# Mixture-of-experts stage: the token scatter, the token gather and the sigmoid issued in other places between the weight steps

## The chip, the cores and the metric

The kernel runs on one core of one Trainium2 chip. Its engines work side by side, each through its own queue in order: TensorE (PE; its weight loads are shown as PEld), VectorE (DVE), ScalarE (ACT), GpSimd (POOL) and SyncE (SP), which here only issues DMAs. The metric is the time of one execution in microseconds, lower is better. All numbers are float32.

## The reference, cut to what matters

One transformer block on 256 tokens of width 2048: a modulated norm, one input projection, two kinds of chunked attention, an output projection, then a two-level mixture of experts and a final modulated norm. The part that the change touches is the mixture:

```python
for e in range(N_EXPERTS):                      # 32 experts, width 512 each
    a = jax.nn.silu(t @ w_gate[e]) * (t @ w_up[e])
    y = y + combine[:, e:e + 1] * (a @ w_down[e])
x = x + gt2 * y
```

Each token has two experts, so `combine` is zero nearly everywhere. The weights of the experts, three matrices of 4 MB for each, are most of what the kernel reads.

## The kernel before

**Weights.** Every large weight goes through one ring of six SBUF buffers of 2 MB (class `Ring`). A list fixes the order of all transfers ahead of time. `release` (called when the last matmul that reads a buffer has been issued in the program) lets SP issue the transfer that takes this buffer next (line 72); on the chip that issue waits until the matmuls have really been done.

**Experts.** They are taken in eight groups of four (line 894). A group has twelve steps of two ring buffers: for J = 0 to 3 a gate step and an up step (`gate_up`, line 773, four experts side by side in four column strips of TensorE), then four down steps fc = 0 to 3 (`down`, line 795). So a group is 24 transfers. Group 7 has eight down steps of one buffer each.

**Around the steps.** Each expert takes 32 slots. `place` (lines 724 and 729, DVE) makes a 0/1 matrix token to slot; `gather` (four `gather_part`s, lines 737 to 748) multiplies the tokens with it on TensorE, and DVE and ACT scale the result into `xg`, the left side of the gate and up matmuls. `activate` (lines 780 to 789) is the gate's silu: exponential on ACT, three operations on DVE, the product with the up result, four transposes on TensorE and a copy by ACT. `gated` (line 804) scales the down result on DVE, `scatter_matrix` (lines 758 to 766) makes the weighted matrix slot to token, and `scatter` (lines 811 and 813) multiplies with it on TensorE and adds into `x1` on DVE.

**Order.** It is written out by hand; every engine follows the order of the program. In each group: the eight gate and up steps, with the whole scatter of the group before behind the two steps of J = 0; then the place and the whole gather of the next group; then `activate`; then the four down steps, `gated` and the `scatter_matrix` of the next group. Group 0 also has `spread` of the gate vector (line 717) and its own `scatter_matrix` ahead of the gather, its scatter at its end, and behind that `further_rounds`, a branch (line 845) that is not taken with these inputs. Its own gather stands in four parts ahead of its first steps. Group 7 has no next group; behind its J = 1 and J = 2 it makes `gscf`, a scale for the final norm (lines 915 to 920). Small results go through a PSUM tag `m` of two banks.

Of the kernel before, what the change touches and what calls it, by code (L numbers as in the profile page):

```python
# [16 lines left out]
F32 = mybir.dt.float32  # L17
I32 = mybir.dt.int32
AF = mybir.ActivationFunctionType
ALU = mybir.AluOpType  # L20
# [21 lines left out]
ROW_ADA, ROW_FIN, ROW_MIX, ROW_FFN, ROW_GFIN, ROW_OA, ROW_OB = 0, 24, 32, 36, 40, 44, 46  # L42
# [42 lines left out]
def block_kernel(ctx: ExitStack, tc: tile.TileContext, a: dict):  # L85
# [72 lines left out]
    pr = const.tile([128, 512], F32, name="pr")  # L158
# [31 lines left out]
    def pick(r, m):  # L190

        return ident[:, r : r + 1].to_broadcast([128, m])
# [25 lines left out]
    with ExitStack() as sa:  # L218
# [181 lines left out]
        def spread(r, dst):  # L400
            for J in range(4):
                pm = bank("m", "pm_bc", 1)
                PE.matmul(pm, lhsT=pick(32 * J, 128), rhs=r, start=True, stop=True)
                S.copy(dst[:, J * 512 : (J + 1) * 512], pm)
# [305 lines left out]
    def mbank(tag, name, bufs):  # L710
        return psb.tile([128, 512], F32, tag=tag, name=name, bufs=bufs)

    def spread(r, row, dst, n=4):

        for J in range(n):
            pm = mbank("m", "bc", 2)
            PE.matmul(pm, lhsT=pick(32 * J, 128), rhs=r, start=True, stop=False)
            PE.matmul(pm, lhsT=pick(row + J, 128), rhs=pr, start=False, stop=True)
            S.copy(dst[:, J * 512 : (J + 1) * 512], pm)
# [12 lines left out]
    def gather_part(xg, pn, q, name):  # L732
        pm = mbank("m", f"g{q}_{name}", 2)
        for i in range(4):
            kk = 4 * q + i
            for t in range(2):
                PE.matmul(  # L737
                    pm[:, i * 128 : (i + 1) * 128], lhsT=big[:, t, kk * 128 : (kk + 1) * 128], rhs=pn[:, t, :],
                    start=t == 0 and i == 0, stop=t == 1, skip_group_check=True,
                )  # L740
        for i in range(4):
            kk = 4 * q + i
            if i % 2:
                S.activation(xg[:, kk, :], pm[:, i * 128 : (i + 1) * 128], AF.Identity, bias=sh2c[:, kk : kk + 1], scale=gsc2[:, kk : kk + 1])  # L744
            else:
                V.tensor_scalar(  # L746
                    xg[:, kk, :], pm[:, i * 128 : (i + 1) * 128], gsc2[:, kk : kk + 1], sh2c[:, kk : kk + 1], op0=ALU.mult, op1=ALU.add
                )

    def gather(pn, name):  # L750
        xg = pb.tile([128, 16, 128], F32, tag="xg", name=f"xg_{name}")
        for q in range(4):
            gather_part(xg, pn, q, name)
        return xg

    def scatter_matrix(pt, cb, name):
        pw = pb1.tile([128, 2, 4, SLOTS], F32, tag="placew", name=f"pw_{name}")
        V.tensor_tensor(pw, pt, cb.unsqueeze(3).to_broadcast([128, 2, 4, SLOTS]), op=ALU.mult)
        return turned(pw.rearrange("p t e c -> p t (e c)"), name)
# [16 lines left out]
                )  # L776

    def activate(gp, up, name):
        act = pb1.tile([128, 512], F32, tag="act", name=f"act_{name}")
        S.activation(act, gp, AF.Exp, scale=-1.0)  # L780
        V.tensor_scalar(act, act, 1.0, None, op0=ALU.add)
        V.reciprocal(act, act)  # L782
        V.tensor_tensor(act, act, gp, op=ALU.mult)  # L783
        V.tensor_tensor(act, act, up, op=ALU.mult)  # L784
        pm = mbank("m", f"at_{name}", 2)
        aT = pb1.tile([128, 4, 128], F32, tag="actT", name=f"actT_{name}")
        for c in range(4):
            PE.transpose(pm[:, c * 128 : (c + 1) * 128], act[:, c * 128 : (c + 1) * 128], ident)  # L788
        S.copy(aT.rearrange("p c n -> p (c n)"), pm)
        return aT  # L790
# [13 lines left out]
            V.tensor_tensor(ys[:, n, :], yp[n], gt2bc[:, c : c + 512], op=ALU.mult)  # L804
        return ys

    def scatter(sm, ys, ch, name, last=False):
        for n in range(2):
            for t in range(2):
                pm = mbank("m", f"sc_{name}{ch}{n}{t}", 2)  # L810
                PE.matmul(pm, lhsT=sm[:, t * 128 : (t + 1) * 128], rhs=ys[:, n, :], start=True, stop=True)  # L811
                c = slice(ch * 1024 + n * 512, ch * 1024 + (n + 1) * 512)
                V.tensor_tensor(x1[:, t, c], x1[:, t, c], pm, op=ALU.add)  # L813
                if last:
                    S.activation(rl, x1[:, t, c], AF.Square, accum_out=ss3[:, t, 2 * ch + n : 2 * ch + n + 1])
                    G.tensor_tensor(big[:, t, c], x1[:, t, c], gscf[:, c], op=ALU.mult)  # L816
# [72 lines left out]

    four = pb1.tile([128, 2], F32, name="four")  # L890
    V.tensor_reduce(four[:, 0:1], ident[:, 0:128:32], axis=AX.X, op=ALU.add)
    xg = pb.tile([128, 16, 128], F32, tag="xg", name="xg_g0")
    gather_part(xg, pn, 0, "g0")
    for g in range(8):
        gu, dn = moe_tiles[g]
        gp, up = mbank("g", f"gp{g}", 1), mbank("u", f"up{g}", 1)
        for J in range(4):
            if g == 0 and J < 3:
                gather_part(xg, pn, J + 1, "g0")
            for i, pbk in ((0, gp), (1, up)):  # L900
                pair = gu[2 * J + i]
                gate_up(pbk, xg, [ring.get(idx) for idx in pair], J)
                for idx in pair:
                    ring.release(idx)
            if J == 0:
                for job in pending:
                    scatter(*job)
                pending = []
            if g == 7 and J >= 1 and J < 3:
                if J == 1:  # L910
                    gscf = pb.tile([128, 16, 128], F32, tag="xg", name="gscf").rearrange("p k n -> p (k n)")
                for b in (2 * J - 2, 2 * J - 1):
                    c = slice(b * 512, (b + 1) * 512)
                    pm = mbank("m", f"gf{b}", 2)
                    PE.matmul(pm, lhsT=pick(ROW_GFIN + b, 128), rhs=pr, start=True, stop=True)
                    S.copy(gscf[:, c], pm)
                    pm = mbank("m", f"sf{b}", 2)
                    PE.matmul(pm, lhsT=pick(32 * b, 128), rhs=R["scf"], start=True, stop=False)
                    PE.matmul(pm, lhsT=pick(ROW_FIN + 4 + b, 128), rhs=pr, start=False, stop=True)
                    V.scalar_tensor_tensor(gscf[:, c], pm, 1.0, gscf[:, c], op0=ALU.add, op1=ALU.mult)  # L920
        if g == 0:
            spread(R["gt2"], ROW_ADA + 20, gt2bc)
            sm = scatter_matrix(pt, comb[:, :, 0:4], "g0")
        if g < 7:
            pt, pn = place(posk[:, :, 4 * g + 4 : 4 * g + 8], f"g{g + 1}")
            xg = gather(pn, f"g{g + 1}")
        aT = activate(gp, up, f"g{g}")
        if g == 7:
            S.activation(four[:, 1:2], four[:, 0:1], AF.Sqrt)
            rl = pb1.tile([128, 512], F32, tag="act", name="rl")  # L930
        if g < 7:
            yp = [mbank("y", f"yp{g}{n}", 4) for n in range(4)]
            for fc in range(4):
                pair = [ring.get(idx) for idx in dn[fc]]
                down(yp, aT, lambda e: pair[e // 2][:, e % 2, :], fc)
                for idx in dn[fc]:
                    ring.release(idx)
            pending = [(sm, gated(yp[2 * ch : 2 * ch + 2], ch, f"g{g}"), ch, f"g{g}") for ch in range(2)]
        else:
            for ch in range(2):  # L940
                yp = [mbank("y", f"yp{g}{ch}{n}", 4) for n in range(2)]
                for fc in range(4):
                    w = ring.get(dn[ch * 4 + fc])
                    down(yp, aT, lambda e: w[:, e, :], fc)
                    ring.release(dn[ch * 4 + fc])
                    if fc == 1 and ch == 1:
                        for job in pending:
                            scatter(*job)
                        pending = []
                    if fc == 1 and ch == 0:  # L950
                        shbc = pb.tile([128, 16, 128], F32, tag="xg", name="shbc").rearrange("p k n -> p (k n)")
                        spread(R["shf"], ROW_FIN, shbc, 2)
                pending.append((sm, gated(yp, ch, f"g{g}"), ch, f"g{g}", True))
        if g < 7:
            sm = scatter_matrix(pt, comb[:, :, 4 * g + 4 : 4 * g + 8], f"g{g + 1}")
        if g == 0:
            for job in pending:
                scatter(*job)
            pending = []
            further_rounds()  # L960
# [67 lines left out]
```

## Time and profile before

| | |
|---|---|
| time, median of 3 runs | 1560.95 us (1560.94 to 1568.42) |
| profiled execution, its time | 1562.42 us |
| its span, first to last instruction | 1560.7 us |
| TensorE matmul busy | 1181.1 us (76%) |
| VectorE busy | 462.6 us (30%) |
| ScalarE busy | 163.8 us (10%) |
| DMA | 599.40 MB, mean 384 GB/s |
| mean granted TensorE clock | 0.891 |

The profile is one execution on the chip. All times inside it count from its first instruction. The granted clock is that of TensorE as a share of 2.4 GHz: 1.00 is that level, 0.50 is 1.2 GHz, and a number between the two means that a stretch held both. A DMA share of 1.00 means that all 16 DMA engines were busy all the time; GB/s says what they moved. Line numbers are those of the kernel before.

### The profile page before, as it was taken

How to read it: one execution, taken by the hardware profiler on the slowest of the kernel's cores; microseconds unless marked ns; L12 is line 12 of the kernel's file. 1: busy time of each engine (PE TensorE's matmuls, PEld its weight loads, DVE VectorE, ACT ScalarE, POOL GpSimd, SP SyncE). 2: the span in 40 equal slices, each digit the busy share in tenths (PEclk: the TensorE clock that was granted, in tenths of full speed). 3: DMA queues.
4: the chain of work that ended last, by engine and by line, in shares of the span. 5: the costliest groups of instructions: out<-in, count | busy, mean ns of one | idle time of the engine just before them, and what ended most of it. 6: DMA issues, size and time to landing. Idle time of an engine off the chain costs nothing.

```text
span 1560.7 us, 14477 instructions
## 1 busy us (share of the span) xinstructions
PE 1181.1 (76%) x6073; PEld 533.7 (34%) x6074; DVE 462.6 (30%) x773; ACT 163.8 (10%) x420; POOL 142.7 (9%) x144
## 2 busy tenths in 40 slices
PE   4999999998989975765567577667657667567866
PEld 1657874873334541311211211211211121131211
DVE  1002667667697730220201201021021022022013
ACT  2101222131310110100100100100000010010001
POOL 0000433332332100000000000000000000000002
PEclk9999999998999988887788888878879888888889
DMA  9999999979799859799999999999999999999998
GB/s 353 390 392 389 352 335 363 373 292 382 300 379 399 332 224 422 313 385 411 422 402 422 421 392 422 421 389 421 421 412 421 421 394 421 422 390 421 421 388 333
DMA packets 128494, 599.40 MB, mean 384 GB/s; under 512 B 5832, under 2 KB 8440, under 8 KB 81064
## 3 DMA queue, kind: packets, MB, share of 16 engines
q1 hardware_dynamic: 124432, 593.51, 95.0%
q10 hardware_dynamic: 3960, 4.88, 0.9%
q8 instruction: 49, 0.80, 0.2%
q14 instruction: 21, 0.17, 0.0%
q0 software_dynamic: 32, 0.02, 0.0%
HBM read 596.02 MB, written 2.12 MB: 383 GB/s over the span
## 4 chain that ended last, share of the span: by engine, by line
DMA 34%; PE 16%; DVE 3%; ACT 1%; issue 0%; SPq 0%; DVEq 0%; ACTq 0%
DMA ring<-w_up 21%; DMA ring<-w_gate 9%; PE yp L795 5%; PE up L773 4%; DMA ring<-w_down 3%; PE gp L773 2%; PE g_g L737 2%; DMA ring<-w_ada_final 1%; DVE act_g L782 1%; ACT xg_g L744 1%; DVE xg_g L746 1%; PE sc_g L811 0%; PE at_g L788 0%; DVE act_g L783 0%; DVE act_g L784 0%
## 5 line engine op out<-in xcount | busy, mean ns | idle before, releaser
L773 PE MATMUL up<-ring,xg_g 128*32 128x512 f32 x1024 | 198.1, 808 | 120.3 <-DMA ring<-w_up 120.3
L773 PE MATMUL gp<-ring,xg_g 128*32 128x512 f32 x1024 | 169.5, 731 | 72.5 <-DMA ring<-w_gate 66.3
L795 PE MATMUL yp<-ring,actT_g 128*32 128x512 f32 x1024 | 156.3, 742 | 53.2 <-DMA ring<-w_down 47.4
L746 DVE TENSOR_SCALAR xg_g<-g_g,gsc,sh2c 128x128 f32<-128x128 f32 x64 | 26.3, 410 | 428.5 <-PE g_g L737 411.5
L773 PEld LDWEIGHTS up<-ring,xg_g 128*32 128x32 f32 x1024 | 43.4, 139 | 266.1 <-DMA ring<-w_up 155.0
L582 PE MATMUL po<-ring,oT 128*128 128x512 f32 x256 | 115.6, 607 | 0.0
L773 PEld LDWEIGHTS gp<-ring,xg_g 128*32 128x32 f32 x1024 | 39.6, 128 | 189.6 <-DMA ring<-w_gate 92.3
L816 POOL TENSOR_TENSOR big<-x,gscf 128x512 f32<-128x512 f32 x8 | 10.0, 1278 | 983.9 <-DVE x L813 983.9
L795 PEld LDWEIGHTS yp<-ring,actT_g 128*32 128x32 f32 x1024 | 36.3, 130 | 167.5 <-issue 91.5
L813 DVE TENSOR_TENSOR x<-x,sc_g 128x512 f32<-128x512 f32 x64 | 44.0, 687 | 152.2 <-PE sc_g L811 152.2
L744 ACT ACTIVATE xg_g<-g_g,sh2c,gsc 128x128 f32<-128x128 f32 x64 | 29.3, 458 | 538.6 <-DVE xg_g L746 538.6
L804 DVE TENSOR_TENSOR ys_g<-yp,gt2bc 128x512 f32<-128x512 f32 x32 | 22.1, 692 | 195.0 <-PE yp L795 195.0
L365 DVE SCALAR_TENSOR_TENSOR acc_gt<-ring,cact,acc_gt 128x1024 f32<-128x1024 f32 x60 | 78.7, 1312 | 1.9
L582 PEld LDWEIGHTS po<-ring,oT 128*128 128x128 f32 x256 | 48.9, 195 | 61.1 <-issue 61.1
L737 PE MATMUL g_g<-pn_g,big 128*128 128x128 f32 x512 | 64.3, 286 | 2.9 <-DVE pn_g L729 1.3
L737 PEld LDWEIGHTS g_g<-pn_g,big 128*128 128x128 f32 x512 | 61.1, 199 | 11.9 <-issue 8.8
L811 PE MATMUL sc_g<-ys_g,smat_g 128*128 128x512 f32 x128 | 61.7, 617 | 0.0
L549 PE MATMUL pw_vB<-ring,hT 128*128 128x512 f32 x128 | 58.4, 614 | 1.5 <-DMA ring<-w_in 1.5
L553 PE MATMUL pw_kB<-hT,ring 128*128 128x256 f32 x256 | 56.6, 381 | 0.0
L553 PE MATMUL pw_qB<-hT,ring 128*128 128x256 f32 x256 | 56.5, 381 | 0.0
L553 PEld LDWEIGHTS pw_qB<-hT,ring 128*128 128x128 f32 x256 | 48.2, 190 | 7.7 <-issue 1.0
L553 PEld LDWEIGHTS pw_kB<-hT,ring 128*128 128x128 f32 x256 | 48.2, 190 | 7.7 <-issue 0.7
(331 smaller groups left out, 1122.6 us busy)
## 6 DMA issues: line engine op xcount, KB each, us to landing
ring<-w_gate SPq DMA_DIRECT2D x64, 2048.0 KB
ring<-w_up SPq DMA_DIRECT2D x64, 2048.0 KB, 20.1
ring<-w_down SPq DMA_DIRECT2D x64, 2048.0 KB, 20.3
ring<-w_ada SPq DMA_DIRECT2D x32, 2048.0 KB, 10.3
ring<-w_in SPq DMA_DIRECT2D x18, 2048.0 KB, 13.0
ring<-w_ada SPq DMA_DIRECT2D x32, 1024.0 KB, 13.8
ring<-w_ada_final SPq DMA_DIRECT2D x15, 2048.0 KB, 8.9
ring<-w_out SPq DMA_DIRECT2D x8, 2048.0 KB, 14.4
```

The costliest lines, as they stand in the source:

```text
L365: V.scalar_tensor_tensor(acc, w[:, kk, :], cact[:, c : c + 1], acc, op0=ALU.mult, op1=ALU.add)
L549: PE.matmul(b[s], lhsT=hT[:, kk, s * 128 : (s + 1) * 128], rhs=w[:, k, :], start=kk == 0, stop=kk == 15)
L553: PE.matmul(b[s][:, n * 256 : (n + 1) * 256], lhsT=w[:, k, c * 128 : (c + 1) * 128], rhs=hT[:, kk, :], start=kk == 0 and n == 0, stop=kk = ...
L582: PE.matmul(b, lhsT=oT[:, (i // 4) * 8 + k, t * 128 : (t + 1) * 128], rhs=w[:, k, :], start=k == 0, stop=k == 7)
L737: PE.matmul(pm[:, i * 128 : (i + 1) * 128], lhsT=big[:, t, kk * 128 : (kk + 1) * 128], rhs=pn[:, t, :], start=t == 0 and i == 0, stop=t == ...
L744: S.activation(xg[:, kk, :], pm[:, i * 128 : (i + 1) * 128], AF.Identity, bias=sh2c[:, kk : kk + 1], scale=gsc2[:, kk : kk + 1])
L746: V.tensor_scalar(xg[:, kk, :], pm[:, i * 128 : (i + 1) * 128], gsc2[:, kk : kk + 1], sh2c[:, kk : kk + 1], op0=ALU.mult, op1=ALU.add)
L773: PE.matmul(bankt[32 * e : 32 * e + 32, :], lhsT=xg[:, kk, 32 * e : 32 * e + 32], rhs=w[e // 2][:, e % 2, j, :], start=kk == 0, stop=kk == ...
L795: PE.matmul(y[32 * e : 32 * e + 32, :], lhsT=aT[:, fc, 32 * e : 32 * e + 32], rhs=w(e)[:, n * 512 : (n + 1) * 512], start=fc == 0, stop=fc ...
L804: V.tensor_tensor(ys[:, n, :], yp[n], gt2bc[:, c : c + 512], op=ALU.mult)
L811: PE.matmul(pm, lhsT=sm[:, t * 128 : (t + 1) * 128], rhs=ys[:, n, :], start=True, stop=True)
L813: V.tensor_tensor(x1[:, t, c], x1[:, t, c], pm, op=ALU.add)
```

## The change

The gather of the next group and the scatter of the last one are issued in pieces, one behind each step, through a list `steps` of twelve entries. For groups 1 to 6 the four quarters of the scatter stand behind steps 0 to 3, `place` behind step 3, the four parts of the gather behind steps 4, 5, 6 and behind the first down step (entry 7). In group 0 the four parts of `spread` stand behind steps 3 to 6, `place` behind step 6, and the gather parts one behind each down step; there is no scatter from a group before. In group 7 the four parts of the final scale stand behind steps 3 to 6. `activate` is cut in two: `silu` stands behind the last gate step, ahead of the last up step; `combined` (product, transposes, copy) stands where `activate` stood. `scatter_matrix` of each group stands at the head of its loop turn; for groups 2 to 7 that is the same place on every engine as before (the end of the turn before), for group 1 it is now behind group 0's scatter and the branch, and for group 0 between the first and the second gather part, ahead of the first gate step. The scatter of group 0 and the branch stay where they were. No operation is added or left out. The core of the diff (`final_scale` holds lines 912 to 920, unchanged):

```diff
+    def new_xg(name):
+        return pb.tile([128, 16, 128], F32, tag="xg", name=f"xg_{name}")
...
     def activate(gp, up, name):
+        return combined(silu(gp, name), up, name)
+
+    def silu(gp, name):
         act = pb1.tile([128, 512], F32, tag="act", name=f"act_{name}")
         S.activation(act, gp, AF.Exp, scale=-1.0)
         V.tensor_scalar(act, act, 1.0, None, op0=ALU.add)
         V.reciprocal(act, act)
         V.tensor_tensor(act, act, gp, op=ALU.mult)
+        return act
+
+    def combined(act, up, name):
         V.tensor_tensor(act, act, up, op=ALU.mult)
...
-    def scatter(sm, ys, ch, name, last=False):
-        for n in range(2):
+    def scatter(sm, ys, ch, name, last=False, ns=(0, 1)):
+        for n in ns:
...
+    after = {}
     for g in range(8):
         gu, dn = moe_tiles[g]
         gp, up = mbank("g", f"gp{g}", 1), mbank("u", f"up{g}", 1)
+        steps = [[] for _ in range(12)]
+        if g:
+            for k, job in enumerate(pending):
+                for n in range(2):
+                    steps[2 * k + n].append(lambda job=job, n=n: scatter(*job, ns=(n,)))
+            pending = []
+        else:
+            for J in range(4):
+                steps[(3, 4, 5, 6)[J]].append(lambda J=J: spread(R["gt2"], ROW_ADA + 20, gt2bc, (J,)))
+        if g < 7:
+            def next_place(g=g):
+                after["place"] = place(posk[:, :, 4 * g + 4 : 4 * g + 8], f"g{g + 1}")
+                after["xg"] = new_xg(f"g{g + 1}")
+
+            def next_gather(q, g=g):
+                gather_part(after["xg"], after["place"][1], q, f"g{g + 1}")
+
+            steps[3 if g else 6].append(next_place)
+            for q in range(4):
+                steps[(4, 5, 6, 7)[q] if g else (7, 8, 9, 10)[q]].append(lambda q=q: next_gather(q))
+        else:
+            gscf = new_xg("gscf").rearrange("p k n -> p (k n)")
+            for b in range(4):
+                steps[3 + b].append(lambda b=b: final_scale(b))
+        sm = scatter_matrix(pt, comb[:, :, 4 * g : 4 * g + 4], f"g{g}")
         for J in range(4):
             if g == 0 and J < 3:
                 gather_part(xg, pn, J + 1, "g0")
...
                 for idx in pair:
                     ring.release(idx)
-            if J == 0:
-                for job in pending:
-                    scatter(*job)
-                pending = []
...
-        if g == 0:
-            spread(R["gt2"], ROW_ADA + 20, gt2bc)
-            sm = scatter_matrix(pt, comb[:, :, 0:4], "g0")
-        if g < 7:
-            pt, pn = place(posk[:, :, 4 * g + 4 : 4 * g + 8], f"g{g + 1}")
-            xg = gather(pn, f"g{g + 1}")
-        aT = activate(gp, up, f"g{g}")
...
+                if J == 3 and i == 0:
+                    act = silu(gp, f"g{g}")
+                if J < 3 or i == 0:
+                    for step in steps[2 * J + i]:
+                        step()
+        aT = combined(act, up, f"g{g}")
         if g < 7:
             yp = [mbank("y", f"yp{g}{n}", 4) for n in range(4)]
             for fc in range(4):
...
                 for idx in dn[fc]:
                     ring.release(idx)
+                for step in steps[7 + fc]:
+                    step()
             pending = [(sm, gated(yp[2 * ch : 2 * ch + 2], ch, f"g{g}"), ch, f"g{g}") for ch in range(2)]
+            pt, pn = after["place"]
+            xg = after["xg"]
...
-        if g < 7:
-            sm = scatter_matrix(pt, comb[:, :, 4 * g + 4 : 4 * g + 8], f"g{g + 1}")
         if g == 0:
             for job in pending:
                 scatter(*job)
```

## Rows read from the trace of the kernel before

**Rows 1.** The page: GB/s in 40 slices of the span; the gate weights' issues.

```profile
GB/s 353 390 392 389 352 335 363 373 292 382 300 379 399 332 224 422 313 385 411 422 402 422 421 392 422 421 389 421 421 412 421 421 394 421 422 390 421 421 388 333
...
ring<-w_gate SPq DMA_DIRECT2D x64, 2048.0 KB
```

**Rows 2.** Stretches by engine; last columns: granted TensorE clock, DMA share, GB/s.

```profile
551.00:571.00 20.00, 15.27 (x107) 9.98 (x107) 8.12 (x44) 2.24 (x6) 0.00 (x0) 0.74 0.14 44
648.00:660.00 12.00, 9.46 (x68) 2.98 (x72) 1.65 (x3) 0.59 (x1) 0.00 (x0) 0.69 0.23 70
698.00:705.00 7.00, 6.62 (x63) 2.56 (x52) 0.00 (x0) 0.00 (x0) 0.00 (x0) 1.00 0.49 151
782.00:787.00 5.00, 5.00 (x52) 1.44 (x48) 0.00 (x0) 0.00 (x0) 0.00 (x0) 1.00 0.75 261
787.00:902.00 115.00, 74.19 (x418) 23.52 (x414) 17.85 (x28) 5.11 (x11) 0.00 (x0) 0.85 1.01 422
902.00:909.00 7.00, 7.00 (x60) 1.79 (x54) 0.00 (x0) 0.00 (x0) 0.00 (x0) 0.82 0.71 250
1024.00:1031.00 7.00, 7.00 (x56) 1.85 (x52) 0.00 (x0) 0.00 (x0) 0.00 (x0) 0.76 0.68 227
1147.00:1152.00 5.00, 5.00 (x52) 1.49 (x48) 0.00 (x0) 0.00 (x0) 0.00 (x0) 1.00 0.92 344
1268.00:1275.00 7.00, 7.00 (x64) 1.90 (x60) 0.00 (x0) 0.00 (x0) 0.00 (x0) 0.88 0.72 260
1389.00:1397.00 8.00, 8.00 (x64) 2.03 (x60) 0.00 (x0) 0.00 (x0) 0.00 (x0) 0.77 0.72 261
1480.00:1524.00 44.00, 28.81 (x160) 7.03 (x152) 6.93 (x7) 3.84 (x6) 0.00 (x0) 0.84 1.01 389
```

**Rows 3.** The chain that ended last: start, us, work.

```profile
876.54 5.33 PE up L773 x28
...
1364.04 5.32 PE up L773 x28
```

**Rows 4.** Timeline of the change from group 2 to 3.

```profile
881.79 7.83 PE L737 MATMUL g_g<-pn_g,big 128*128 128x128 f32 x64
...
891.40 0.59 ACT L780 ACTIVATE act_g<-gp 128x512 f32<-128x512 f32 x1
...
897.43 1.09 PE L788 MATMUL at_g<-ident,act_g 128*128 128x128 f32 x4 [7.81 <-DVE act_g L784]
...
899.25 13.09 PE L795 MATMUL yp<-ring,actT_g 128*32 128x512 f32 x96 [0.73 <-ACT actT_g L789]
...
905.51 0.88 SPq L72 DMA_DIRECT2D ring<-w_down  x2
```

**Rows 5.** Timeline of the start of group 0.

```profile
557.55 6.49 PE L737 MATMUL g_g<-pn_g,big 128*128 128x128 f32 x32 [1.30 <-DVE pn_g L729]
...
562.40 0.41 DVE L746 TENSOR_SCALAR xg_g<-g_g,gsc,sh2c 128x128 f32<-128x128 f32 x1 [0.65 <-ACT xg_g L744]
...
563.96 3.64 PE L773 MATMUL gp<-ring,xg_g 128*32 128x512 f32 x32
...
567.63 0.88 SPq L72 DMA_DIRECT2D ring<-w_up  x2
```

**Rows 6.** One microsecond of that start, columns as in rows 2.

```profile
563.00:564.00 1.00, 1.00 (x13) 0.88 (x13) 0.00 (x0) 0.31 (x1) 0.00 (x0) 0.92 0.00 0
```

**Rows 7.** End of group 0: scatter, gate step, weight issue, branch of line 845.

```profile
677.77 7.81 PE L811 MATMUL sc_g<-ys_g,smat_g 128*128 128x512 f32 x16
...
691.71 5.89 PE L773 MATMUL gp<-ring,xg_g 128*32 128x512 f32 x32 [6.12 <-DVE pn_g L729]
...
701.65 0.89 SPq L72 DMA_DIRECT2D ring<-w_up  x2
...
L845 PEldq COMPARE_BRANCH  x1: 6192/6192/6192, 685.1 to 685.1; - x1
```

**Rows 8.** Gate matmuls of all groups; ns of one: least, median, most.

```profile
L773 PE MATMUL gp<-ring,xg_g x1024: 589/593/1062, 564.0 to 1481.0; 128*32 128x512 f32 x171
```

More of the change, by code (lines that the diff above doesn't have):

```diff
@@ L711, in mbank, with spread @@
         return psb.tile([128, 512], F32, tag=tag, name=name, bufs=bufs)
-    def spread(r, row, dst, n=4):
-        for J in range(n):
+    def spread(r, row, dst, js=range(4)):
+        for J in js:
             pm = mbank("m", "bc", 2)
@@ L750, in gather @@
     def gather(pn, name):
-        xg = pb.tile([128, 16, 128], F32, tag="xg", name=f"xg_{name}")
+        xg = new_xg(name)
         for q in range(4):
@@ L891, in block_kernel, with final_scale @@
     V.tensor_reduce(four[:, 0:1], ident[:, 0:128:32], axis=AX.X, op=ALU.add)
-    xg = pb.tile([128, 16, 128], F32, tag="xg", name="xg_g0")
+    xg = new_xg("g0")
     gather_part(xg, pn, 0, "g0")
+    def final_scale(b):
+        c = slice(b * 512, (b + 1) * 512)
+        pm = mbank("m", f"gf{b}", 2)
+        PE.matmul(pm, lhsT=pick(ROW_GFIN + b, 128), rhs=pr, start=True, stop=True)
+        S.copy(gscf[:, c], pm)
+        pm = mbank("m", f"sf{b}", 2)
+        PE.matmul(pm, lhsT=pick(32 * b, 128), rhs=R["scf"], start=True, stop=False)
+        PE.matmul(pm, lhsT=pick(ROW_FIN + 4 + b, 128), rhs=pr, start=False, stop=True)
+        V.scalar_tensor_tensor(gscf[:, c], pm, 1.0, gscf[:, c], op0=ALU.add, op1=ALU.mult)
+    after = {}
     for g in range(8):
@@ L904, in block_kernel @@
                     ring.release(idx)
-            if J == 0:
-                for job in pending:
-                    scatter(*job)
-                pending = []
[L909 to L920, printed above, removed]
-        if g == 0:
-            spread(R["gt2"], ROW_ADA + 20, gt2bc)
-            sm = scatter_matrix(pt, comb[:, :, 0:4], "g0")
-        if g < 7:
-            pt, pn = place(posk[:, :, 4 * g + 4 : 4 * g + 8], f"g{g + 1}")
-            xg = gather(pn, f"g{g + 1}")
-        aT = activate(gp, up, f"g{g}")
-        if g == 7:
-            S.activation(four[:, 1:2], four[:, 0:1], AF.Sqrt)
-            rl = pb1.tile([128, 512], F32, tag="act", name="rl")
+                if J == 3 and i == 0:
[4 more added lines that the diff above has]
+        aT = combined(act, up, f"g{g}")
         if g < 7:
@@ L937, in block_kernel @@
                     ring.release(idx)
+                for step in steps[7 + fc]:
+                    step()
             pending = [(sm, gated(yp[2 * ch : 2 * ch + 2], ch, f"g{g}"), ch, f"g{g}") for ch in range(2)]
-        else:
+            pt, pn = after["place"]
+            xg = after["xg"]
+        else:
+            S.activation(four[:, 1:2], four[:, 0:1], AF.Sqrt)
+            rl = pb1.tile([128, 512], F32, tag="act", name="rl")
             for ch in range(2):
@@ L950, in block_kernel @@
                     if fc == 1 and ch == 0:
-                        shbc = pb.tile([128, 16, 128], F32, tag="xg", name="shbc").rearrange("p k n -> p (k n)")
-                        spread(R["shf"], ROW_FIN, shbc, 2)
+                        shbc = new_xg("shbc").rearrange("p k n -> p (k n)")
+                        spread(R["shf"], ROW_FIN, shbc, range(2))
                 pending.append((sm, gated(yp, ch, f"g{g}"), ch, f"g{g}", True))
-        if g < 7:
-            sm = scatter_matrix(pt, comb[:, :, 4 * g + 4 : 4 * g + 8], f"g{g + 1}")
         if g == 0:
```

## The prediction

> **What bounds the kernel now.** The first thing to read is the page's line of GB/s [rows 1]. From about the sixteenth of the 40 slices on, where the experts run, most slices stand at 421 or 422, with a weaker slice at each change of group (389 to 412). So the experts are bound by DMA, and the only time that an edit of the compute can win there is time in which the DMA engines had nothing to do. The second view is the table of stretches [rows 2]. Between the weak spots the rate is 422 GB/s at a DMA share of 1.01. The weak spots are short: one at the end of group 0's up steps (648 to 660 us, 70 GB/s), one at each of the six changes from group 1 to 2 up to 6 to 7 (782 to 787, 902 to 909 and so on), one at the branch (698 to 705), and one ahead of group 0 (551 to 571, share 0.14).
>
> I count a hole by its missing bytes, as the width times (1 - rate/422), because a DMA that has been issued but moves nothing yet shows as busy. The hole of group 0 is 12 x (1 - 70/422) = 10.0 us. The six changes are 1.9, 2.9, 3.2, 0.9, 2.7 and 3.1 us, together 14.7. Counted by the DMA share they would be 9.2 and 10.1; that is the low end. A check from another view: in the chain of waits the last up step of group 2 starts at 876.54 and that of group 6 at 1364.04 [rows 3], so four groups take 487.5 us, 121.9 each. A group moves 24 transfers of 2048 KB [rows 1], 50.33 MB, at 422 GB/s 119.3 us. The 2.6 us between agree with the holes (mean 2.4); six times 2.6 is 15.6, the high end.
>
> What makes a hole is to be read in the timeline of one change [rows 4]. The last up step ends at 881.8. Then TensorE does the whole gather, 64 matmuls in 7.8 us. ACT can start the silu's exponential only behind the gather's last scaling, at 891.40; the transposes come at 897.43 and the first down step at 899.25. For 17.5 us no ring buffer is released. The issue that the first down step releases comes at 905.51, while the ring's outstanding transfers have run out at about 903: a hole of 2.9 us.
>
> **The change part by part.** *The changes of group 1 to 6.* Between the last up and the first down step remain the product with the up result, the transposes and the copy. The rows give 899.25 - 897.43 = 1.8 us for transposes and copy; with the product, one of the five operations in the 6.0 us from 891.40 to 897.43 and under 1 us of them, it is under 2.8 us instead of 17.5. The first down step then waits for its own weights. All moved work goes into the steps' slack: a step must keep to the 9.95 us in which its two buffers arrive (119.3/12). Its 32 matmuls take 3.64 us at 2.4 GHz [rows 5], some 7.3 at 1.2 (an estimate, twice as long). A gather part is 7.83/4 = 2.0 us, a scatter quarter 7.81/4 = 2.0 us [rows 4, 7]. That is 5.6 us with one piece, and 9.3 with the matmuls of the step at half clock. The DVE and ACT work of the pieces stands behind no release: the ring waits only for TensorE's matmuls, and each SP issue stands in the program ahead of the piece. In step 6 the silu stands on DVE ahead of the gather part's scaling (some 5 of those 6.0 us), but the up step reads neither result, and the gather part writes the PSUM bank that the one before last has left, a step earlier. So all six holes should go: -14.7 us (-10.1 to -15.6). If the cover were gone, by more than 20 us of delay (four outstanding buffers), they would come back.
>
> *Group 0's hole.* `spread`, scatter matrix, gather and silu stood in one row here, 25 us. They go behind steps 3 to 6 and behind the down steps in the same way, with the same slack: -10.0 us (-9.2 to -10.0).
>
> *The start of group 0, the cost.* `scatter_matrix` now stands between the first and second gather part. Ahead of group 0 all six buffers are full and DMA stands still until the first gate step ends; the issue came at 567.63 [rows 5]. So each microsecond here is one of the total. TensorE did both gather parts in one piece, 557.55 to 564.04 (3.25 us each, the first at 1.2 GHz), then the gate from 563.96 to 567.6. Now its two transposes wait for `pw` on DVE, which stands behind the scaling that starts at 562.40 and takes 0.41: `pw` (about as long, an estimate from that row) is done at 563.3, the transposes at 563.8. The second gather part then ends at 567.1 at half clock, at 565.8 at full clock. At half clock throughout, the gate takes 7.3 us and ends at 574.4, +6.8 us; at full clock throughout it ends at 569.4, +1.8. The clock rose in the microsecond from 563 [rows 6], when TensorE had worked without a pause since 557.55. Now it pauses from 560.8 to 563.3, so the rise may come later: I take the middle, +4.3, and keep both ends. The same transposes and `spread` at group 0's end are counted in its hole.
>
> *The end of group 0.* The last gather part (2.0 us) and its scaling (1.4) now stand ahead of `gated`, whose four products no longer overlap the down step, and `scatter_matrix` for group 1 stands behind the branch (0.5). I make the scatter's end, then the branch of 6.2 us on TensorE [rows 7], then group 1's first gate step some 3 to 4 us later against the weights' arrival than before. But SP's next issue came at 701.65, though TensorE's gate step had left that buffer at 697.6: the hole of 4.5 us at the branch (7 x (1 - 151/422)) ends with SP. I read it so that SP leaves the branch only when its outstanding transfers have landed. Those 4.0 us hide the delay: 0, bounded by +1.5. The hole itself stays.
>
> *Group 7.* No hole stands at its change to the down steps (389 GB/s at share 1.01 from 1480 to 1524 [rows 2]): its silu was already early. Moving the scale pieces puts 2.8 us more into steps with the same slack: 0. The tail follows the last transfers and moves with them.
>
> The sum: -14.7 - 10.0 + 4.3 + 0 = -20.4 us on the profiled execution's 1562.42, giving 1542.0. The median of the runs shown is 1.5 us below the profiled one: **1540.5 us**. The ends: -15.6 - 10.0 + 1.8 = -23.8 gives 1537; -10.1 - 9.2 + 6.8 + 1.5 = -11.0 gives 1550.
>
> **The rivals.** *TensorE at 1.2 GHz becomes the bound; slower.* The long gather and the 96 down matmuls behind it are the stretch in which TensorE works without a gap; cut into pieces, each step ends in a wait for weights. If the clock then stayed at half, groups 1 to 7 would be paced by TensorE. The longest single gate matmul takes 1062 ns against 593 in the median [rows 8]; four run side by side, so a step of 32 would be 8.5 us at that length, twelve steps 102. With gather 13.0 (four times 3.25) and scatter 15.6 (twice 7.8) and some 6 for the change, that is 137 us a group instead of 121.9; seven groups cost 103 us, and with group 0's hole and start (-5.7) the time is 1658. It decides from about 124 us a group, a step of 7.4 us, where seven times 1.9 us outweigh the -5.7 by 0.5% of the time. Against it: with 7.3 us a step the group is 122, no loss; and the stretch from 787 to 902 holds a mean grant of 0.85 though its steps already end in waits for weights [rows 2]; more work in the same time leaves shorter gaps. 5%. The Trainium skill ("TensorE: Matmul & The Clock Gate", section "HAM oscillation — how this bites in real kernels") says that waits for data between bursts of matmuls throttle the clock again and advises keeping the work in one piece; by that rule the change leans towards the 1658 and without it stays at the forecast. The row with 0.85 shows both levels within a group already.
>
> *Half of the gain.* The holes shrink but do not close, because a piece lengthens a step that already ran late, or the start costs the most. With the six holes halved and the start at +6.8 the sum is -7.4 - 10.0 + 6.8 = -10.6, 1550.4. For it: the steps 3 and 6 carry two or three pieces. Against it: 20 us of outstanding transfers. 13%.
>
> *It does not do what it says.* If the releases, not the gather, were late by SP's own issue, moving TensorE's work would change nothing but group 0's start: +4.3, 1565.3, inside 0.5%. Against it: SP's issue at 905.51 comes 6.3 us behind the start of the down steps, with the end of the first of the four. 7%.
>
> **How the numbers follow.** The forecast has 75%. Faster by over 0.5% (7.8 us, about what a measurement can tell from no change) holds the forecast and most of the halved gain: 0.87. Same 0.08, slower 0.05. The range 1536 to 1551 takes in the forecast's ends and the halved gain.
>
> **What would show it.** In the changed profile: no stretch under 400 GB/s between 575 us and group 7 but the one at the branch; from last up to first down step no more than about 5 us; a group period of 119.3 to 120 us; the first weight issue of group 0 some 4 us later against the first gather matmul. It is wrong if holes stand at new places, above all behind steps 3 or 6, if the granted clock of a group falls towards 0.5 with the period above 122, or if the hole at the branch grows beyond 6 us.

## The result and the profile after

| | before | after |
|---|---|---|
| time, median | 1561.9 us (4 runs, 1560.94 to 1568.42) | 1540.42 us (4 runs, 1539.71 to 1540.73) |
| profiled execution | 1562.42 us | 1540.73 us |
| its span | 1560.7 us | 1539.0 us |
| mean granted TensorE clock | 0.891 | 0.912 |

The ratio is 0.9853, with a 95% interval of 0.9825 to 0.9881: faster by 1.5%. The time lies 0.1 us from the predicted 1540.5, which is closer than the terms deserve, as the point-by-point part shows.

The page of the kernel after, GB/s in 40 slices, answers to [rows 1]:

```profile
GB/s 353 390 392 383 385 328 346 375 290 391 319 348 397 353 162 423 421 409 387 422 422 422 421 422 422 421 422 421 421 421 421 421 422 422 421 421 421 420 401 323
```

The list has 40 slices; from the sixteenth on, the weaker ones at the group changes are gone. What is left is the start of group 0 (162, the fifteenth slice), the branch across two slices (409 and 387) and the tail. The stretches of the kernel after, with columns as in [rows 2]:

```profile
550.00:573.00 23.00, 16.09 (x108) 10.73 (x108) 8.69 (x47) 2.62 (x7) 0.00 (x0) 0.70 0.11 33
573.00:690.00 117.00, 84.70 (x474) 30.11 (x474) 19.94 (x35) 9.39 (x19) 0.00 (x0) 0.91 1.01 422
690.00:697.00 7.00, 7.00 (x60) 1.84 (x56) 0.00 (x0) 0.00 (x0) 0.00 (x0) 0.85 0.49 160
697.00:820.00 123.00, 83.04 (x486) 24.90 (x478) 14.20 (x21) 5.22 (x11) 0.00 (x0) 0.85 1.01 422
820.00:940.00 120.00, 86.02 (x476) 25.81 (x472) 17.77 (x28) 5.22 (x11) 0.00 (x0) 0.87 1.01 421
940.00:1060.00 120.00, 85.00 (x470) 25.86 (x466) 17.77 (x28) 5.22 (x11) 0.00 (x0) 0.84 1.01 421
1060.00:1180.00 120.00, 84.20 (x486) 25.50 (x478) 17.77 (x28) 5.21 (x11) 0.00 (x0) 0.90 1.01 421
1180.00:1300.00 120.00, 84.34 (x472) 25.66 (x470) 17.76 (x28) 5.22 (x11) 0.00 (x0) 0.86 1.01 421
1300.00:1420.00 120.00, 83.98 (x474) 25.42 (x470) 17.77 (x28) 5.21 (x11) 0.00 (x0) 0.89 1.01 421
1460.00:1500.00 40.00, 26.65 (x158) 7.21 (x154) 7.14 (x7) 4.43 (x7) 0.00 (x0) 0.93 1.02 401
```

All stretches from 697 to 1420 us, which hold the six changes from group 1 to 7, stand at 421 or 422 GB/s. The end of group 0's up steps, 70 GB/s for 12 us before, lies inside the row from 573 to 690 and has vanished. The hole at the branch is 7 x (1 - 160/422) = 4.3 us, as before (4.5). The stretch ahead of group 0 has grown from 20 to 23 us. Group 7's start of the down steps (1460 to 1500) runs at 401 GB/s with a share of 1.02. By missing bytes that is 40 x (1 - 401/422) = 2.0 us; before, by [rows 2], it was 44 x (1 - 389/422) = 3.4.

The chain that ended last of the kernel after (start, us, work), answering to [rows 3]; both are the second down step, of group 2 and of group 6:

```profile
887.08 3.65 PE yp L804 x28
...
1366.79 5.35 PE yp L804 x28
```

Four groups take 479.7 us, 119.9 each, against 121.9 before and 119.3 at 422 GB/s. Here is one change, from group 2 to 3, in the timeline of the kernel after, to be read beside [rows 4]:

```profile
867.68 2.75 PE L776 MATMUL up<-ring,xg_g 128*32 128x512 f32 x20
...
870.47 0.69 DVE L793 TENSOR_TENSOR act_g<-act_g,up 128x512 f32<-128x512 f32 x1 [0.50 <-PE up L776]
...
871.31 0.63 PE L797 MATMUL at_g<-ident,act_g 128*128 128x128 f32 x4 [0.88 <-DVE act_g L793]
...
872.66 1.05 PE L804 MATMUL yp<-ring,actT_g 128*32 128x512 f32 x4 [0.73 <-ACT actT_g L798]
...
876.74 5.16 PE L804 MATMUL yp<-ring,actT_g 128*32 128x512 f32 x28 [3.02 <-DMA ring<-w_down]
...
881.83 2.05 PE L737 MATMUL g_g<-pn_g,big 128*128 128x128 f32 x16
```

The last up step ends at 870.4, the product starts at once, the transposes at 871.31, and the first down step at 872.66: a pause of 2.2 us where it was 17.5. From there TensorE waits for weights (3.0 us ahead of 876.74), where before the weights' buffers waited for TensorE, and a gather part of 2.05 us stands behind the step. The granted clock of the stretches above from 820 on is 0.84 to 0.90, against 0.85 in the stretch of before from 787 to 902.

### The profile page after: what moved, and what is told of

It reads as the page before. It is cut to its first block, busy times and chain, and to the rows that moved or that the text cites. A ratio compares the mean times of both kernels' runs of the same rounds, so it can differ in the third digit from the quotient of the medians.

```text
span 1539.0 us, 14488 instructions
## 1 busy us (share of the span) xinstructions
PE 1196.3 (78%) x6073; PEld 529.9 (34%) x6074; DVE 461.6 (30%) x773; ACT 164.7 (11%) x420; POOL 142.8 (9%) x144
## 4 chain that ended last, share of the span: by engine, by line
DMA 46%; PE 8%; issue 0%; DVE 0%; DVEq 0%; SPq 0%
DMA ring<-w_gate 21%; DMA ring<-w_down 13%; DMA ring<-w_up 11%; PE gp L776 4%; PE up L776 2%; PE yp L804 2%; DMA ring<-w_ada_final 1%; PE tail L1025 0%; PE part L1020 0%; PE tail L1030 0%; DVE big L1033 0%; DVEq L1057 0%; SPq L72 0%; PE gf L908 0%; DVEq L1033 0%
## 5 line engine op out<-in xcount | busy, mean ns | idle before, releaser
L804 PE MATMUL yp<-ring,actT_g 128*32 128x512 f32 x1024 | 182.2, 765 | 108.5 <-DMA ring<-w_down 102.7
L776 PE MATMUL up<-ring,xg_g 128*32 128x512 f32 x1024 | 178.7, 726 | 79.9 <-DMA ring<-w_up 79.9
L776 PEld LDWEIGHTS up<-ring,xg_g 128*32 128x32 f32 x1024 | 38.9, 128 | 205.5 <-DMA ring<-w_up 114.3
L825 POOL TENSOR_TENSOR big<-x,xg_gscf 128x512 f32<-128x512 f32 x8 | 10.0, 1278 | 962.4 <-DVE x L822 962.4
L737 PE MATMUL g_g<-pn_g,big 128*128 128x128 f32 x512 | 68.5, 289 | 1.3 <-DVE pn_g L729 1.3
```

What stands on the lines that cost most here:

```text
L737: PE.matmul(pm[:, i * 128 : (i + 1) * 128], lhsT=big[:, t, kk * 128 : (kk + 1) * 128], rhs=pn[:, t, :], start=t == 0 and i == 0, stop=t == ...
L776: PE.matmul(bankt[32 * e : 32 * e + 32, :], lhsT=xg[:, kk, 32 * e : 32 * e + 32], rhs=w[e // 2][:, e % 2, j, :], start=kk == 0, stop=kk == ...
L804: PE.matmul(y[32 * e : 32 * e + 32, :], lhsT=aT[:, fc, 32 * e : 32 * e + 32], rhs=w(e)[:, n * 512 : (n + 1) * 512], start=fc == 0, stop=fc ...
```

## The experiments

Two numbers order what follows. I call **pause** the time between the end of the last up step and the first down step, in which no ring buffer comes free, and **hole** the missing bytes at the rate of 422 GB/s. In the kernel before, a pause of 17.5 us left holes of 2.4 us on the mean, and group 0's pause of 25.1 us one of 10.0. In both, the hole is about 15 us shorter than the pause. If the hole is only what the pause has over that, the gain doesn't add up from the parts of the change: each move that brings the pause under 15 us earns all of it, and a second one nothing. The rival theory is that each part earns its share of the pause. The kernel before had medians of 1564.5, 1561.3 and 1566.4 us in the three sets of runs below, so times are compared within a set, and by ratio.

**The silu late, the pieces kept.**

```diff
-                if J == 3 and i == 0:
-                    act = silu(gp, f"g{g}")
...
+        act = silu(gp, f"g{g}")
         aT = combined(act, up, f"g{g}")
```

> The changed kernel with the silu whole behind the last up step again, all pieces as changed. Theory (a hole is the pause without a release, from the last up to the first down step, less what the ring still has outstanding; the pause of 17.5 us left 2.4 us of hole on the mean, so pauses under some 15 us leave none): the pause becomes about 8.5 us, no hole, the time stays at that of the changed kernel, 1540 us, within 1. Rival (the silu's early place earns a share of the gain of its own, by its part of the pause, 6 of 17.5 us): a third of the 24.7 us comes back, 1548.

1541.03 us, ratio to before 0.9849 (0.9829 to 0.9868). The experts' groups 1 to 6 as one stretch of this kernel, and rows of group 3:

```profile
697.00:1420.00 723.00, 509.09 (x2841) 154.41 (x2834) 103.58 (x161) 30.61 (x66) 0.00 (x0) 0.86 1.01 421
```

```profile
984.53 0.59 ACT L786 ACTIVATE act_g<-gp 128x512 f32<-128x512 f32 x1
...
989.00 0.69 DVE L789 TENSOR_TENSOR act_g<-act_g,gp 128x512 f32<-128x512 f32 x1
...
990.94 0.69 DVE L793 TENSOR_TENSOR act_g<-act_g,up 128x512 f32<-128x512 f32 x1 [1.26 <-PE up L776]
...
993.13 1.05 PE L804 MATMUL yp<-ring,actT_g 128*32 128x512 f32 x4 [0.73 <-ACT actT_g L798]
```

No hole, but no long pause either: the expected 8.5 us did not come. The silu is late in the program only. It reads nothing of the up step, so ACT and DVE do it from 984.53 to 989.7, before the last up step is done (990.9). The pause is 2.2 us here and in most groups, 4.6 to 4.7 in groups 1 and 2. In the kernel before, the silu was late because it stood behind the scaling of the whole gather [rows 4]. So this run does not test what a late silu costs; it shows that with the gather in pieces the silu's place in the program hardly matters.

**The gather whole, the silu early.**

```diff
-            steps[3 if g else 6].append(next_place)
-            for q in range(4):
-                steps[(4, 5, 6, 7)[q] if g else (7, 8, 9, 10)[q]].append(lambda q=q: next_gather(q))
+            whole = [next_place] + [lambda q=q: next_gather(q) for q in range(4)]
...
+        if g < 7:
+            for step in whole:
+                step()
         aT = combined(act, up, f"g{g}")
```

> The changed kernel with place and gather in one piece behind the last up step again, the silu early, scatter and spread in pieces. Theory: the pause becomes about 12.5 us in all of groups 0 to 6, still under 15, so no hole: 1540 us, at most 1542. Rival (each part earns by its share of the pause): the gather is the larger part, 9 of 17.5 us, so about half of the gain comes back, 1552.

1539.93 us, ratio 0.9843 (0.9823 to 0.9862). The same stretch, and the change from group 2 to 3:

```profile
696.00:1420.00 724.00, 499.28 (x2815) 154.50 (x2816) 103.84 (x164) 31.27 (x66) 0.00 (x0) 0.84 1.01 421
```

```profile
870.58 7.82 PE L737 MATMUL g_g<-pn_g,big 128*128 128x128 f32 x64
...
881.89 8.34 PE L804 MATMUL yp<-ring,actT_g 128*32 128x512 f32 x60 [0.73 <-ACT actT_g L798]
```

The gather begins as the last up step ends, and the first down step comes 11.2 us later (12.5 expected). Again no hole, although 9 of the 15 us that the change took out of the pause are back. By its share of the pause this run would have lost about half of the gain: that rival is refuted.

**Both at their old places**, the two edits together:

> The changed kernel with both at their old places; only scatter, spread and group 0's scatter matrix stay as changed. Theory: the pause is 17.5 us again in groups 0 to 6, the six holes come back (14.7 us) and group 0 has one like them (2.4) in place of 10: 1540.4 + 17 = 1557.5. Rival (shares add): the losses of the two runs before, 8 and 12, add to 20: 1560, and by this rival the single runs have shown their parts; by the theory they have shown nothing.

1558.38 us (8 runs, 1556.42 to 1560.94), ratio 0.996 (0.9945 to 0.9974). Four of its seven holes:

```profile
650.00:656.00 6.00, 6.00 (x60) 1.60 (x56) 0.00 (x0) 0.00 (x0) 0.00 (x0) 0.92 0.63 220
777.00:783.00 6.00, 6.00 (x59) 1.56 (x52) 0.00 (x0) 0.00 (x0) 0.00 (x0) 0.98 0.69 227
1144.00:1151.00 7.00, 7.00 (x60) 1.83 (x56) 0.00 (x0) 0.00 (x0) 0.00 (x0) 0.87 0.60 215
1391.00:1395.00 4.00, 4.00 (x40) 1.19 (x36) 0.00 (x0) 0.00 (x0) 0.00 (x0) 1.00 0.88 354
```

The first is group 0's, 6 x (1 - 220/422) = 2.9 us, where it was 10.0 before: with `spread` in pieces its pause is that of the other groups. The six changes hold 16.5 us together. Here the silu stands behind the whole gather's scaling again, and the pause is 17.3 to 17.5 us. So two edits whose single runs stand within 0.7 us of the kernel after cost 18 us together: singly the pause was at most 4.7 and 11.3 us. The theory of shares can't give that: by the prices of the single runs the time would have been near 1540.

**One line's move in the kernel before**: the silu early, nothing else (`activate` is split into `silu` and `combined` as in the change).

```diff
...
                 for idx in pair:
                     ring.release(idx)
+                if J == 3 and i == 0:
+                    act = silu(gp, f"g{g}")
...
-        aT = activate(gp, up, f"g{g}")
+        aT = combined(act, up, f"g{g}")
```

> The kernel before with one part of the change: the silu behind the last gate step. Theory: the pause of groups 1 to 6 falls from 17.5 to 12.5 us, so all six holes go (-14.7); group 0's pause falls from 25.2 to about 20, so its hole falls from 10 to 5 us; the start costs nothing more. 1561.5 - 19.7 = 1542, nearly the whole gain by one line moved. Rival (shares): -8 us, 1553.

1541.05 us, ratio 0.9845 (0.9825 to 0.9866): the whole gain in one move, within what the runs can tell apart. The one hole left besides the branch is group 0's:

```profile
650.00:656.00 6.00, 6.00 (x60) 1.66 (x56) 0.00 (x0) 0.00 (x0) 0.00 (x0) 0.99 0.58 176
```

It is 6 x (1 - 176/422) = 3.5 us (5 expected), after a pause of 19.0 us; in groups 1 to 6 the pause is 11.2 to 11.3. What this kernel loses there it saves at the start of group 0, which costs nothing more here.

**Group 0's scatter matrix later.**

```diff
-        sm = scatter_matrix(pt, comb[:, :, 4 * g : 4 * g + 4], f"g{g}")
+        if g:
+            sm = scatter_matrix(pt, comb[:, :, 4 * g : 4 * g + 4], f"g{g}")
...
+                if g == 0 and J == 1 and i == 1:
+                    sm = scatter_matrix(pt, comb[:, :, 0:4], "g0")
                 if J < 3 or i == 0:
                     for step in steps[2 * J + i]:
```

> The changed kernel with group 0's scatter matrix behind its fourth step instead of ahead of its first. Theory (it delays the first release by 3.0 us, and DMA stands still there): the first weight issue comes 10.1 us behind the first gather matmul instead of 13.1, and the time falls by 3.0 us to 1537.4. Rival (the delay is taken back, because the branch at the end of group 0 drains the transfers anyway): the issue is earlier but the time stays at 1540.4.

1536.66 us (6 runs, 1535.87 to 1538.37), ratio 0.9843 (0.9815 to 0.9871); the kernel with the scatter whole (below), which behaves like the one after, had 1540.61 (1537.68 to 1541.44) in the same set. The interval of the ratio overlaps with that of the kernel after; what stands firmly is the timeline of the start:

```profile
555.65 6.45 PE L737 MATMUL g_g<-pn_g,big 128*128 128x128 f32 x32 [1.29 <-DVE pn_g L729]
...
565.70 0.88 SPq L72 DMA_DIRECT2D ring<-w_up  x2
```

From the first gather matmul to the first weight issue it takes 10.05 us, as before the change (10.08), against 13.07 in the kernel after. The difference of the two spans is 4.6 us; 1.2 of it lies ahead of group 0, which no edit touched, so 3.4 remain for the 3.0 of the start.

**Without the branch**: the call of `further_rounds` is taken out, and with it what it would do for experts with more tokens than slots.

```diff
             pending = []
-            further_rounds()
```

> The changed kernel without the branch behind group 0 and what it guards (further rounds for experts with more tokens than slots, of which there are none here). Theory: the hole of 4.4 us at the branch goes, because SP no longer waits for its outstanding transfers to land: 1536.0. Rival (the hole is TensorE's, late by the branch and by the scatter ahead of it): half of it stays, 1538 or more, with a weak stretch between 685 and 700 us.

1537.00 us (6 runs, 1534.91 to 1538.21), ratio 0.9844 (0.9816 to 0.9872), 3.6 us below 1540.61 in the same set. The stretch in which the branch stood:

```profile
660.00:720.00 60.00, 44.56 (x244) 14.49 (x242) 11.02 (x21) 2.45 (x6) 0.00 (x0) 0.83 1.01 421
```

The hole is gone altogether, although the scatter ahead of it is as it was. The rival, by which half of it would stay with TensorE's late scatter, falls. The branch on TensorE's own queue went with it, so this run doesn't part SP's wait from TensorE's.

**The scatter whole**, behind the second step:

```diff
-                    steps[2 * k + n].append(lambda job=job, n=n: scatter(*job, ns=(n,)))
+                    steps[1].append(lambda job=job, n=n: scatter(*job, ns=(n,)))
```

> The changed kernel with the four quarters of the scatter in one piece behind the second step. Theory: there the step takes 7.8 us longer at most, the ring has some 15 us outstanding, no hole: 1540.4, within 0.7. Rival (pieces smooth the steps and win by that): slower by 2 us or more with holes behind the second step of groups 2 to 7.

1540.61 us (6 runs), ratio 0.9863 (0.9835 to 0.9892).

```profile
697.00:1420.00 723.00, 501.21 (x2823) 152.16 (x2812) 104.41 (x163) 31.31 (x66) 0.00 (x0) 0.87 1.01 421
```

Cutting the scatter is worth nothing: its 7.8 us are under the 15 in one piece as well.

**A ring of five buffers**, in the kernel before and in the one after (`RING = 5`), one run each. This takes the 15 us themselves for a test: one buffer less is 5 us less outstanding.

> The kernel before with a ring of five buffers instead of six; its stages ahead of the experts use the same ring and may move too, so only the stretch of the experts counts. Theory: the outstanding transfers shrink by one, 5 us, so pauses over some 10 us leave holes: six of 7.4 us instead of 2.4 and group 0's 15 instead of 10; the experts take 35 us longer. Rival (the holes are TensorE's pace or SP's issue, not the ring's depth): holes as before, the experts' stretch unchanged.

1604.96 us. Three of the seven holes of before with five buffers, group 0's first:

```profile
646.00:663.00 17.00, 8.93 (x56) 2.73 (x60) 5.60 (x6) 1.99 (x4) 0.00 (x0) 0.70 0.13 40
786.00:796.00 10.00, 9.27 (x60) 2.50 (x62) 0.00 (x0) 0.59 (x1) 0.00 (x0) 0.64 0.26 79
1168.00:1180.00 12.00, 11.27 (x72) 3.07 (x71) 0.00 (x0) 0.59 (x1) 0.00 (x0) 0.68 0.28 91
```

By missing bytes group 0's is 17 x (1 - 40/422) = 15.4 us (15 expected), and the six changes sum to 46.2, 7.7 each (7.4 expected). Each hole has grown by some 5 us, the time of one transfer. That the pace of TensorE or SP's own issue makes the holes is refuted: neither was touched. From the first weight issue of group 0 (565.93) to the end of the span (1603.2) this kernel takes 1037.3 us, 44 more than the kernel before, where 35 were expected: the seven holes give 37, one transfer more (5) has to be moved behind that issue, and the branch, group 7 and the tail hold the rest.

> The changed kernel with a ring of five buffers; only the stretch of the experts counts, as in the run of the kernel before with five. Theory: with a pause of some 3 us between last up and first down step no hole appears in groups 0 to 6 even with 5 us less outstanding; the experts' stretch keeps 421 GB/s but for the branch. Rival (the steps with pieces are near their limit, which six buffers cover up): holes behind the steps with pieces, 10 us or more in all.

1553.37 us. Two stretches of after with five buffers at full rate, its one hole, and what stood there:

```profile
575.00:692.00 117.00, 84.34 (x460) 29.51 (x452) 18.78 (x31) 9.01 (x18) 0.00 (x0) 0.90 1.01 422
692.00:705.00 13.00, 10.67 (x70) 2.76 (x70) 1.24 (x4) 0.37 (x1) 0.00 (x0) 0.74 0.39 133
825.00:945.00 120.00, 83.91 (x473) 25.67 (x471) 18.13 (x29) 5.21 (x11) 0.00 (x0) 0.89 1.01 421
```

```profile
L854 SPq EVENT_SEMAPHORE  x9: 17/17/17, 676.2 to 695.8; - x9
```

```profile
694.73 5.80 PE L776 MATMUL gp<-ring,xg_g 128*32 128x512 f32 x32
...
700.56 0.38 SPq L72 DMA_DIRECT2D ring<-w_gate  x1
```

No hole in any change of group, also not behind the steps with pieces. The hole at the branch has doubled, 13 x (1 - 133/422) = 8.9 us; that was not expected, but the rows say why. SP is done with the branch at 695.8, the gate step that frees the next buffer only at 700.5, and the issue follows at once. With six buffers the gate step ended just ahead of SP (see the branch below); here it ends 4.7 us behind, and by that much the hole has grown. The time is 12.6 us above that of six buffers: 4.5 lie there, the first issue of group 0 comes 2.3 us later, and 5.0 are one transfer that with one buffer less had not been loaded ahead of group 0 (2.1 MB more are moved behind that issue). The rest lies in the tail.

**Two moves only**: silu early, and `spread` in pieces with group 0's matrix behind the fourth step; gather and scatter whole.

> Of the change only two moves: the silu early, and spread in pieces with group 0's scatter matrix behind its fourth step; gather and scatter in one piece as before. Theory: pauses of about 12.5 us, no hole in any group, start as before: 1537, the same as with all pieces and the later matrix. Rival (the pieces of gather and scatter are worth something beyond the pause): 1540 or more.

1538.05 us (5 runs, 1535.01 to 1540.26), ratio 0.9829 (0.9806 to 0.9852). Its span is 1534.3 us, that of the kernel with all pieces and the later matrix 1534.4. Both have the shortest spans of all kernels here that keep the branch; the pauses are 11.2 to 11.3 us with two moves and 2.2 with all pieces. By spans and ratios the pieces of gather and scatter are worth nothing beyond the pause, though one of the five runs lies at the 1540 that the rival named. Their lead on the kernel after, 4.6 and 4.7 us of span, is 0.3%, and in the ratios the intervals overlap.

## Why the prediction was right, point by point

**The bound and the holes: right.** The experts ran at 421 to 422 GB/s before and after, and what was won is the missing bytes. From the first weight issue of group 0 to the end of the span the kernel before takes 1560.7 - 567.63 = 993.1 us and the one after 1539.0 - 569.88 = 969.1: 24.0 us less, against 24.7 forecast for the seven holes. Counting a hole by its bytes was the better choice; by the DMA share it would have been 19.3. The forecast put group 7 at nothing because of its share; by bytes 1.4 us were won there, and the tail lost about 1. The group period came out at 119.9 (119.3 to 120 named).

**The pause: right in the mechanism, with one consequence not drawn.** The prediction has the pause fall from 17.5 to under 2.8 us; it is 2.2. It also says that the holes come back from more than 20 us of delay, four outstanding buffers. Counted from the end of the last up step to the release by the first down step, that measure holds: in the change of [rows 4] this is 905.5 - 881.8 = 23.7 us, which less the hole of 2.9 leaves 20.8, and four transfers of 5.0 us are 20. Over the seven changes of the kernel before the cover so counted is 20.7 to 22.3 us, with five buffers 14.6 to 16.3. Counted as a pause it is about 15, because the pause leaves out the first down step. That step takes 5.7 to 6.5 us in the six changes, and with it the holes differ, from 0.9 to 3.2 us, though the six pauses are equal within 0.1.

What the prediction did not draw from its own rows is how little has to go: the pause of 17.5 us needs to be cut by about 3, not by 15. The silu early alone did it, and so did the gather in pieces with the silu at its old place in the program. So the change looks like several improvements and is, at the group changes, one that was paid for twice; the pieces of the scatter add nothing there. In group 0 both the silu and `spread` count, because the pause there was 25 us.

**The start of group 0: right in sign and place, too large.** Forecast +4.3, measured 13.07 - 10.08 = +3.0. The timeline of the kernel after, to be read beside [rows 5], and the granted clock of that time, with columns as in [rows 2]:

```profile
556.81 3.75 PE L737 MATMUL g_g<-pn_g,big 128*128 128x128 f32 x16 [1.30 <-DVE pn_g L729]
...
562.00 0.42 DVE L761 TENSOR_TENSOR pw_g<-pl_g,comb 128x256 f32<-128x256 f32 x1
...
562.47 0.29 PEld L767 LDWEIGHTS sm_g<-ident,pw_g 128*128 128x128 f32 x2 [2.20 <-DVE pw_g L761]
...
562.95 3.33 PE L737 MATMUL g_g<-pn_g,big 128*128 128x128 f32 x16
...
566.22 3.64 PE L776 MATMUL gp<-ring,xg_g 128*32 128x512 f32 x32
...
569.88 0.88 SPq L72 DMA_DIRECT2D ring<-w_up  x2
```

```profile
562.00:566.00 4.00, 3.53 (x17) 3.53 (x18) 0.42 (x2) 0.83 (x2) 0.00 (x0) 0.52 0.00 0
566.00:567.00 1.00, 1.00 (x11) 0.38 (x13) 0.41 (x1) 0.23 (x1) 0.00 (x0) 1.00 0.00 0
```

TensorE stands still behind the first gather part, the transposes wait for `pw` (562.00 to 562.42) and start at 562.47, and the second gather part takes 3.3 us at 1.2 GHz: all this as laid out. The gate step then takes 3.64 us at 2.4 GHz. The clock was half until shortly before 566, when TensorE had worked again since 562.47; the term failed in putting both pieces of work midway between the two levels. The whole gate step was at the upper level, 1.8 us less than the middle, and the gather part at the lower, 0.65 us more; together that is 1.2 of the 1.3 us.

**The branch: right.** The forecast has the delay of TensorE hidden behind SP's wait, and no change in the hole. Here are the branch's instructions of the kernel after on SP and on TensorE's queue (count, ns of one, first and last start), and those of the kernel before on SP:

```profile
L854 SPq EVENT_SEMAPHORE  x9: 17/17/17, 668.7 to 693.5; - x9
L854 PEldq COMPARE_BRANCH  x1: 5912/5912/5912, 679.8 to 679.8; - x1
```

```profile
L845 SPq EVENT_SEMAPHORE  x9: 17/17/17, 678.2 to 701.2; - x9
```

SP's last one stands at 693.5 (701.2 before), the next weight issue at 693.96 (701.65 before), while the last transfers issued ahead of the branch end in the holes that begin at 690 and 698. The first five of SP's nine start at 668.7, 673.3, 678.3, 683.3 and 688.3, the other four from 693.3 on: they are 4.6 to 5.0 us apart, the pace at which the transfers land. The gate step that frees the buffer ends at 693.2: counted from the landing of the last down weights (669.76 before, 663.27 after) that is 29.9 us against 27.8, 2.1 us later, where 3 to 4 were named. It stays 0.3 us short of SP's last instruction, so the cover held, but only just; with five buffers it was gone, and the hole grew by what the gate step came later. That SP's part is a wait for its transfers is inferred from these times, from the run without the branch and from the one with five buffers; no run took that wait away alone.

**The rivals.** TensorE at half clock as the bound didn't come: the granted clock of the groups is 0.84 to 0.90, the period 119.9. Its price of 8.5 us a step, from the longest single matmul, was too high as well: in the kernel before, the first down step from 1021.5 to 1028.0 took 6.5 us at a granted clock of 0.55. The Trainium skill ("TensorE: Matmul & The Clock Gate", section "HAM oscillation — how this bites in real kernels") advises, for matmuls that come in bursts between waits for data, doing the work in one piece. This stage does not bear that out: its waits stood there anyway, and in the stretch from about 697 to 1420 us the clock is 0.84 with the gather whole and 0.86 and 0.87 in the two runs above with the gather in pieces. Half of the gain, from steps with several pieces, didn't come either: not even five buffers show a hole behind them. Nor was SP's own issue the cause: the holes went with TensorE's work alone.

**Why the number is closer than its terms.** On the profiled execution the forecast was 1542.0 and 1540.73 came. The start was 1.3 us cheaper and the stages ahead of group 0, which the change doesn't touch, 0.7 us shorter; the stretch behind the first issue won 0.7 us less than the sum of the holes. The 1.3 us that are left vanish in the step from the profiled execution to the median: the forecast took 1.5 off, and it was 0.3. That the two cancel is luck.

## What to carry to other kernels

In a stage bound by DMA with a ring of buffers, set the longest time between two releases against what the ring still has outstanding, counting the step that ends in the next release. Only the excess is lost, and it is lost in full. One move that brings the time under that measure earns everything, and further ones only give margin, which counts when the ring gets shorter. Before work is cut into pieces, look for the cheapest move that takes the excess away, and keep what is moved clear of places where the transfers already stand still. And a line moved in the program is not always work moved on the chip: whether an edit has moved the wait that it is to test shows in the timeline.

## What the runs showed of the hardware that was not expected

A branch that is not taken leaves a hole in the transfers: 4.3 to 4.5 us in the kernels before and after, none without the branch. SP issues nothing from the branch until about when the transfers outstanding there have landed (inferred from the times above). The hole can also end with TensorE. With a ring one buffer shorter it was 8.9 us in the kernel after, where the gate step that frees the next buffer ended 4.7 us behind SP's last instruction of the branch, and 7 x (1 - 116/422) = 5.1 in the one before, where it ended 1.0 us behind. The compare-and-branch on TensorE's queue took 5.9 us (6.2 before), against 0.05 to 0.07 us on SP, ACT and DVE; what it does in that time the traces don't say.
